# Low parts of the weights formed half a piece later, side tasks cut into shorter steps, sigmoids written as tanh in a one-core decoder trunk

## The chip, the cores and the metric

The kernel runs on one core of a Trainium2 chip. The metric is the device time of an execution in microseconds (us). In what follows PE is the matmul engine (PEld its weight loads), DVE the vector engine, ACT the scalar engine, POOL and SP the two engines that here mostly issue transfers. Each engine works through its own instructions in the order in which the program wrote them, and waits where an instruction needs what another engine has not finished.

## The reference

One layer of a hybrid decoder trunk on 256 tokens of width 2048, all in float32:

```python
hn = rms_norm(h, ln_gain)
z = split_columns(hn @ w_in + b_in)                # 2048 x 15904 weights
y_a = rglru_branch(z['lru_x'], ...) * silu(z['lru_gate'])
y_b = nsa_branch(...) * silu(z['nsa_gate'])        # sparse attention, 8 heads
y_c = fox_branch(...) * silu(z['fox_gate'])        # forgetting attention, 8 heads
mg = sigmoid(z['merge'])
merged = mg[0] * (y_a @ w_branch[0]) + mg[1] * (y_b @ w_branch[1]) + mg[2] * (y_c @ w_branch[2])
h = h + merged @ w_out
h = h + sigmoid(h @ w_ple_gate) * rms_norm(p @ w_ple, ple_gain)
```

The recurrence of the first branch, per channel, is what one part of the change rewrites:

```python
rec = sigmoid(ub @ wa + ba);  inp = sigmoid(ub @ wx + bx)
log_a = -8 * rec * softplus(-lam);  a = exp(log_a)
drive = sqrt(-expm1(2 * log_a)) * (inp * uc)
hseq[t] = a[t] * hseq[t-1] + drive[t]
```

## The kernel before

The time goes into streaming all weights through PE once. `plan()` cuts them into 384 pieces of 128 x 1024 numbers (some are 816 or 544 wide). For each piece, in the order of the plan:

- SP issues its transfer into one of `RAW` = 5 buffers `raw` (`issue`), up to `LOADS` = 6 pieces ahead in the program; a transfer waits until the buffer's earlier piece has been read.
- `cut` splits it for matmuls in a reduced float format (float32r): ACT copies it into the high part `wh`, DVE subtracts and writes the low part `wl`. Both have `AHEAD` + 1 = 4 buffers, so `wh` of piece i+3 can be written once PE has finished with piece i-1. `cut` is called at the start of piece i for piece i+3.
- `by_rows` gives PE twelve matmuls of 512 columns (`mm3`: activations' high part by `wh`, by `wl`, and their low part by `wh`; two row tiles, two contraction steps). The results build up in four PSUM tiles `main`.

Everything else (the recurrence, norms, turning of tiles, both attentions, the products with gates, the splits of their results) is written as Python generators, the side tasks: `lru_task`, `nsa_task`, `fox_task`, `y_split` and others. `Side.tick()` lets each running task emit its instructions up to its next `yield`; it is called in the middle of a piece's matmuls (in `by_rows`) and at the end of each piece. A tick stops when the planner's own clock puts DVE or ACT further behind PE than `LIMITS` allows. So the order on each engine is fixed when the program is built, and the side tasks' instructions stand between the `wh` and `wl` instructions of successive pieces. Side tasks' matmuls write four PSUM tiles `bank`; the last of them end at about 639 us, and after that only gates, splits and norms are left beside the weights.

Names used below: `k_lru` are the recurrence's tiles, `spc` and `spn` columns of its constants, `k_zt` a turned tile, `k_mg` the merge gate (formed by DVE from `main`, then a tanh on ACT, right after a merge chunk's last piece), `k_yh` and `k_yl` the split of a branch's result that the next product's matmuls read, `k_fx` the split of one forgetting head's query and key. A helper (line 206) records every operation, so all rows of the trace carry L206.

Of the kernel before, what the change touches and what calls it, by code (L numbers as in the profile page):

```python
# [12 lines left out]
AF = mybir.ActivationFunctionType  # L13
OP = mybir.AluOpType
# [309 lines left out]
def block_kernel(ctx: ExitStack, tc: tile.TileContext, io):  # L324
# [81 lines left out]
            Q.dma_start(h["raw"][:, a:b],  # L406
                        bass.AP(tensor=wsrc.tensor, offset=wsrc.offset + h["off"] + a, ap=[[m, P], [1, b - a]]))

    def cut(h, k=0, nk=None):
        m, n = h["nk"] * h["n"], h["n"]  # L410
        nk = nk or h["nk"]
        if k == 0:
            h["whl"] = [wp.tile([P, 1024], R32, tag=x, bufs=AHEAD + 1, name=nm(x)) for x in ("wh", "wl")]
        wh, wl = h["whl"]
        for a, b in parts_of(h, k, nk):
            split(wh[:, a:b], wl[:, a:b], h["raw"][:, a:b])
        h["wh"] = wh[:, :m].rearrange("p (k n) -> p k n", n=h["n"])
        h["wl"] = wl[:, :m].rearrange("p (k n) -> p k n", n=h["n"])

# [7 lines left out]
    def by_rows(h, x):  # L427

        if h["first"]:
            turn[0] ^= 1  # L430
            turns[h["kind"], h.get("what"), h["key"]] = turn[0]
        n = h["n"]
        out = [mains[2 * turn_of(h) + t][:, :n] for t in range(NT)]
        steps = [(h, t, k) for t in range(NT) for k in range(h["nk"])]
        if h is halves[0] or h is halves[1]:
            steps.sort(key=lambda x: x[2])
        if h is halves[-2]:
            return out
        if h is halves[-1]:

            steps = [(g, t, k) for t in range(NT) for g in halves[-2:] for k in range(g["nk"])]
        if h is halves[0]:

            (hi, lo), cuts = x(0), parts_of(h, 0, 1)
            for ws, last in (("wh", 0), ("wl", 1)):
                for a, b in cuts:
                    for t in range(NT):
                        T.matmul(out[t][:, a:b], hi[:, t * P:(t + 1) * P], h[ws][:, 0, a:b],
                                 start=a == 0 and not last, stop=False)
            for t in range(NT):  # L450
                T.matmul(out[t], lo[:, t * P:(t + 1) * P], h["wh"][:, 0, :], start=False, stop=False)
            steps = steps[NT:]
        for j, (g, t, k) in enumerate(steps):
            ts = slice(t * P, (t + 1) * P)
            if 2 * j == len(steps):
                side.tick()
            hi, lo = x(g["k"] + k)
            mm3(out[t], hi[:, ts], lo[:, ts], g["wh"][:, k, :], g["wl"][:, k, :], g["first"] and k == 0,
                g["last"] and k == g["nk"] - 1)
        return out  # L460
# [127 lines left out]
            split(hi[:, k, :], lo[:, k, :], x_tile(2 * i + k), x0[:, S + 2 * i + k:S + 2 * i + k + 1])  # L588

    def vec_task():  # L590
        a = VEC["lru_gate"]
        V.tensor_scalar(vec[:, a:], vec[:, a:], 0.5, None, op0=OP.mult)
        nl = sml([P, 8], name="nl")
        V.tensor_scalar(nl, vec[:, VEC["lam"]:VEC["lam"] + 8], -1.0, None, op0=OP.mult)
        yield from softplus(spc, nl, 8)
        V.tensor_scalar(spn, spc, -8.0, None, op0=OP.mult)
        V.tensor_scalar(spc, spc, 8.0, None, op0=OP.mult)

        V.scalar_tensor_tensor(gqn, vcol("nq"), SCALE, vcol("nk"), op0=OP.mult, op1=OP.mult)
        V.scalar_tensor_tensor(gqf, vcol("fq"), SCALE, vcol("fk"), op0=OP.mult, op1=OP.mult)  # L600
        yield True
# [123 lines left out]
    def lru_task(i):  # L725
        yield from side.wait("vec", f"lru_x{i // 2}")
        yield from side.room(k2=4, k4=1)
        u = st["u"]
        uc = two([P, 2, S], name="uc")


        ucs = [two([P, 2, S], R32, name="ucs") for _ in range(2)]
        wd = two([P, 2, 2, P], name="wd")
        G.dma_start(wd, io["wd"][:, 2 * i:2 * i + 2])
        for c in range(2):
            ct = 2 * i + c
            V.tensor_scalar(uc[:, c, :], u[:, ct, :], vcol("conv_w", 4 * ct + 3), vcol("conv_b", ct),
                            op0=OP.mult, op1=OP.add)
            for s in (1, 2, 3):
                V.scalar_tensor_tensor(uc[:, c, s:], u[:, ct, :S - s], vcol("conv_w", 4 * ct + 3 - s),  # L740
                                       uc[:, c, s:], op0=OP.mult, op1=OP.add)
            yield True
        own, other = (slice(0, 64), slice(64, P)), (slice(64, P), slice(0, 64))
        for c in range(2):
            for s in range(2):
                A.activation(ucs[c][own[s], s, :], uc[own[s], c, :], AF.Copy)
            for s in range(2):
                V.tensor_tensor(ucs[c][other[s], s, :], uc[own[s], c, :], f(ucs[c][own[s], s, :]), op=OP.subtract)
            yield True
        wds = mid([P, 2, 2, 2, P], R32, name="wds")  # L750
        wdh, wdl = wds[:, 0], wds[:, 1]
        split(wdh, wdl, wd)
        yield from side.settle()
        bs = yield from side.take(2)
        for c in range(2):
            for s in range(2):

                g = banks[bs[c]][:, s * S:(s + 1) * S]
                T.matmul(g, wdh[:, c, s, :], ucs[c][:, s, :], start=True, stop=False)
                T.matmul(g, wdl[:, c, s, :], ucs[c][:, s, :], start=False, stop=True)  # L760
        side.give(k4=1)
        yield True
        rec, inp, th = (two([P, 2, S], name="lru") for _ in range(3))
        for c in range(2):
            ct = 2 * i + c
            for s in range(2):
                g = banks[bs[c]][:, s * S:(s + 1) * S]
                A.activation(rec[own[s], c, :], g[own[s]], AF.Sigmoid, bias=vcol("ba", ct)[own[s]])
                A.activation(inp[own[s], c, :], g[other[s]], AF.Sigmoid, bias=vcol("bx", ct)[other[s]])
        side.back(*bs)  # L770
        yield True
        for c in range(2):
            ct = 2 * i + c
            A.activation(th[:, c, :], rec[:, c, :], AF.Tanh, scale=spc[:, ct:ct + 1])
        for c in range(2):
            ct = 2 * i + c
            A.activation(rec[:, c, :], rec[:, c, :], AF.Exp, scale=spn[:, ct:ct + 1])
        V.tensor_tensor(inp, inp, uc, op=OP.mult)
        yield True

        A.activation(uc, rec, AF.Square)
        V.scalar_tensor_tensor(th, uc, 1.0, th, op0=OP.add, op1=OP.mult)
        yield True
        A.activation(th, th, AF.Sqrt)
        V.tensor_tensor(th, th, inp, op=OP.mult)
        yield True
        for c in range(2):
            V.tensor_tensor_scan(st["yl"][:, 2 * i + c, :], rec[:, c, :], th[:, c, :], 0.0, op0=OP.mult, op1=OP.add)
        side.give(k2=4)
        yield True  # L790
# [106 lines left out]
    def nsa_task(g, pr, t):  # L897
# [19 lines left out]
        def soft(a, sc):  # L917

            for i, (o, x, msk) in enumerate(zip((pc[:, a, :], ps[:, a, 0, :], ps[:, a, 1, :]), sc,
                                                (cmask[:, t, :], mask[:, P * (2 - n):2 * P], mask[:, P:P + n * P]))):  # L920
                V.tensor_tensor_reduce(o, x, msk, -1.0, FLOOR, OP.add, OP.min, m[:, a, i:i + 1])
            for i, (o, x) in enumerate(((pc[:, a, :], pc[:, a, :]), (cell[:, a, 0], cells(ps[:, a, 0, :])),
                                        (cell[:, a, 1], cells(ps[:, a, 1, :])))):
                A.activation(o, x, AF.Exp, bias=m[:, a, i:i + 1], scale=-1.0, accum_out=s[:, a, i:i + 1])

        if t == 0:
# [3 lines left out]
            yield True  # L930
            for a in range(2):
                x = banks[bs[a]]
                soft(a, (x[:, 128:144], x[:, 144:272], x[:, :128]))
                side.back(bs[a])
                yield True
        else:
            for a in range(2):
# [1 line left out]
                mm3(banks[b0][:, :272], qh[:, a, :], ql[:, a, :], kh[:, g, :272], kl[:, g, :272], True, True)  # L939
                mm3(banks[b1][:, :256], qh[:, a, :], ql[:, a, :], kh[:, g, 272:], kl[:, g, 272:], True, True)  # L940
                yield True
                soft(a, (banks[b0][:, 256:272], banks[b1][:, :256], banks[b0][:, :256]))
                side.back(b0, b1)
                yield True
        side.give(k1=2)
# [4 lines left out]
        for a in range(2):  # L950
            V.tensor_scalar(pc3[:, a, :].rearrange("p (i c) -> p i c", i=3)[:, :, :16],
                            pc[:, a, None, :].to_broadcast([P, 3, 16]), s[:, a, 0:1], None, op0=OP.mult)
            for w in range(2):
                V.tensor_scalar(cell[:, a, w], cell[:, a, w], s[:, a, 1 + w:2 + w], None, op0=OP.mult)
        pt = pz.rearrange("p b n j -> p (b n j)")
        yield from cross(pt, pt, p)
        side.give(**{size: 1})
# [304 lines left out]
    def prepare(j):  # L1262
# [12 lines left out]
    for i, h in enumerate(halves):  # L1275
# [36 lines left out]
        else:  # L1312
            kv = h["key"]
            if h["first"] and kv == 0:
                st["cmpb"] = side.free.pop(0)[0]
            for k in range(h["nk"]):
                for q, w in enumerate((h["wh"], h["wl"])):
                    T.matmul(banks[st["cmpb"]][:4 * NCMP, kv * HID:(kv + 1) * HID], st["xs"][kv][:, h["k"] + k, :],
                             w[:, k, :], start=h["first"] and k == 0 and q == 0 and kv == 0,
# [21 lines left out]
        if halves[min(i + 3, len(halves) - 1)]["kind"] == "ple" and "pTs" not in st:  # L1341
            st["pTs"] = pTh, pTl = two([P, 2, S], R32, name="pTh"), two([P, 2, S], R32, name="pTl")
            split(pTh, pTl, st["pT"])
        for name in h["starts"]:
            start(name)
        side.tick()
# [14 lines left out]
MARGIN = 1600.0  # L1361

LAND = 5500.0
LIMITS = ((3500.0, 2500.0), (4000.0, 3500.0))

CMP_FROM = 17

# [74 lines left out]
```

## Time and profile before

| | us |
|---|---|
| median of 3 runs (1073.91 to 1074.62) | 1074.49 |
| the profiled execution | 1074.18 |
| its span, first to last instruction | 1072.4 |
| PE busy | 1059.0 |
| DVE busy | 771.2 |
| ACT busy | 617.4 |

Matmuls are pipelined: one of 512 columns shows as 0.39 us of busy time, and the next one starts before it ends. So PE is marked idle only where a matmul comes later than the drain of the one before it, and the distance from start to start tells more than the idle time. The granted clock is 1.0 of full speed in every stretch of work.

### The profile page before, as it was taken

To read this page: it belongs to the slowest core of one execution; us is meant where nothing else is said; L and a number is where in the kernel's file an instruction comes from. 1 tells how busy PE (TensorE), PEld (TensorE's weight loads), DVE (VectorE), ACT (ScalarE), POOL (GpSimd) and SP (SyncE) were. 2 spreads that over 40 slices of the span, in tenths; PEclk is the share of its full clock that TensorE was granted. 3 is DMA by queue.
4 is the path that set the end of the run, shared out by engine and by line. 5 is a ranking of instruction groups with operands and counts; after the bars stand their busy time and mean duration, and the time that the engine had idled before them with its cause. 6 is when DMAs were issued, how large, how long until landed. Compare 5 with 4: busy or idle time off the path is not lost.

```text
span 1072.4 us, 14101 instructions
## 1 busy us (share of the span) xinstructions
PE 1059.0 (99%) x4943; PEld 881.2 (82%) x4943; DVE 771.2 (72%) x1139; ACT 617.4 (58%) x917; POOL 51.1 (5%) x77
## 2 busy tenths in 40 slices
PE   9999999999999999999999999999999999999998
PEld 7887789887878878887888888888888888888886
DVE  7777699877787777778886866555776567666664
ACT  7668986776665565645645544465555444444442
POOL 0000000000000000001010000000000100000000
PEclk9999999999999999999999999999999999999999
DMA  9757768776666667558676776766676876788762
GB/s 340 251 186 220 255 219 266 243 240 193 214 206 195 198 200 221 159 172 281 201 224 210 226 217 184 236 216 204 206 255 199 264 248 212 228 253 262 264 215 79
DMA packets 86151, 237.54 MB, mean 222 GB/s; under 512 B 14008, under 2 KB 31040, under 8 KB 86080
## 3 DMA queue, kind: packets, MB, share of 16 engines
q1 hardware_dynamic: 81360, 220.89, 63.4%
q0 software_dynamic: 4720, 15.76, 5.7%
q8 instruction: 38, 0.62, 0.2%
q14 instruction: 33, 0.27, 0.1%
HBM read 215.62 MB, written 4.20 MB: 205 GB/s over the span
## 4 chain that ended last, share of the span: by engine, by line
PE 89%; ACT 4%; DVE 3%; DMA 2%; issue 2%; SPq 0%; DVEq 0%; ACTq 0%
PE main L206 85%; PE bank L206 4%; DVE wl L206 2%; ACT wh L206 2%; ACT k_lru L206 1%; DMA raw<-in_w 1%; DMA k_zn<-k_zt 1%; ACT L206 1%; SPq L206 0%; DVE k_zn L206 0%; ACT k_yh L206 0%; DVE k_fq L206 0%; DVE k_qn L206 0%; DVE k_zt L206 0%; DVE k_fin L206 0%
## 5 line engine op out<-in xcount | busy, mean ns | idle before, releaser
L206 DVE TENSOR_TENSOR wl<-raw,wh 128x1024 fp32r<-128x1024 f32 (+2 forms) x388 | 459.2, 1199 | 235.5 <-ACT wh L206 234.3
L206 ACT ACTIVATE wh<-raw 128x1024 fp32r<-128x1024 f32 (+2 forms) x388 | 397.9, 1039 | 291.3 <-PE main L206 258.4
L206 PE MATMUL main<-wh,k_hnh 128*128 128x512 f32 (+2 forms) x1026 | 395.8, 386 | 1.8 <-ACT wh L206 1.7
L206 PE MATMUL main<-wl,k_hnh 128*128 128x512 f32 (+2 forms) x1026 | 393.5, 384 | 3.4 <-DVE wl L206 3.3
L206 PE MATMUL main<-wh,k_hnl 128*128 128x512 f32 (+1 forms) x1024 | 392.7, 384 | 0.0
L206 PEld LDWEIGHTS main<-wl,k_hnh 128*128 128x128 f32 x1026 | 192.6, 188 | 41.6 <-DVE wl L206 6.5
L206 PEld LDWEIGHTS main<-wh,k_hnh 128*128 128x128 f32 x1026 | 193.0, 188 | 39.4 <-ACT wh L206 3.8
L206 PEld LDWEIGHTS main<-wh,k_hnl 128*128 128x128 f32 x1024 | 192.3, 188 | 37.7
L206 PE MATMUL main<-wl,k_yh 128*128 128x512 f32 x192 | 75.0, 391 | 1.0 <-DVE wl L206 1.0
L206 PE MATMUL main<-wh,k_yh 128*128 128x512 f32 x192 | 75.1, 391 | 0.5 <-ACT k_yh L206 0.5
L206 PE MATMUL main<-wh,k_yl 128*128 128x512 f32 x192 | 75.0, 390 | 0.0
L206 PE MATMUL main<-wh,k_mtl 128*128 128x512 f32 x128 | 49.9, 389 | 0.0
L206 PE MATMUL main<-wh,k_hth 128*128 128x512 f32 x128 | 49.8, 389 | 0.0
L206 PE MATMUL main<-wh,k_mth 128*128 128x512 f32 x128 | 49.8, 389 | 0.0
L206 PE MATMUL main<-wl,k_mth 128*128 128x512 f32 x128 | 49.8, 389 | 0.0
L206 PE MATMUL main<-wl,k_hth 128*128 128x512 f32 x128 | 49.8, 389 | 0.0
L206 PE MATMUL main<-wh,k_htl 128*128 128x512 f32 x128 | 49.8, 389 | 0.0
L206 PEld LDWEIGHTS main<-wl,k_yh 128*128 128x128 f32 x192 | 36.1, 188 | 9.0 <-DVE wl L206 1.7
L206 PEld LDWEIGHTS main<-wh,k_yh 128*128 128x128 f32 x192 | 36.1, 188 | 8.4 <-ACT k_yh L206 0.9
L206 PEld LDWEIGHTS main<-wh,k_yl 128*128 128x128 f32 x192 | 36.1, 188 | 7.9 <-DVE k_yl L206 0.4
L206 ACT ACTIVATE k_mg<-k_mg 128x512 f32<-128x512 f32 x24 | 15.2, 633 | 29.5 <-DVE k_mg L206 29.1
L206 PEld LDWEIGHTS main<-wh,k_htl 128*128 128x128 f32 x128 | 24.0, 188 | 5.0
(240 smaller groups left out, 957.0 us busy)
## 6 DMA issues: line engine op xcount, KB each, us to landing
raw<-in_w SPq DMA_DIRECT2D x369, 512.0 KB, 4.4
bias<-in_b_in POOLq DMA_DIRECT2D x21, 256.0 KB, 4.8
raw<-in_w SPq DMA_DIRECT2D x8, 408.0 KB, 3.8
k_pz<-k_prob SPq DMA_DIRECT2D x16, 128.0 KB, 3.9
e_dram<-k_e POOLq DMA_DIRECT2D x4, 512.0 KB, 3.7
k_merged<-k_zt SPq DMA_DIRECT2D x16, 128.0 KB, 2.9
k_xc<-in_x POOLq DMA_DIRECT2D x4, 512.0 KB, 5.2
k_hx<-k_zt SPq DMA_DIRECT2D x16, 128.0 KB, 3.0
```

What stands on the lines that cost most here:

```text
L206: r = call(out, *args, **kw)
```

## The change

Four edits. (1) From piece 14 on, `cut` emits ACT's copy at once but puts DVE's subtraction into a list `due`, which `low_parts()` empties in the middle of a piece, after the tick there, and at the end of each piece. (2) The recurrence's two sigmoids become tanh of half the argument, with the factors folded into `spc`, `spn`, the biases and the square root, and the sequence that read them is adapted. (3) Three more `yield`s cut the steps of `lru_task` and `nsa_task`, and one bank is given back earlier. (4) The second pair of `LIMITS` goes from (4000, 3500) to (3000, 2500).

```diff
+    due = []
+    def low_parts():
+        while due:
+            V.tensor_tensor(*due.pop(0), op=OP.subtract)
-    def cut(h, k=0, nk=None):
+    def cut(h, k=0, nk=None, late=False):
...
-            split(wh[:, a:b], wl[:, a:b], h["raw"][:, a:b])
+            if late:
+                A.activation(wh[:, a:b], h["raw"][:, a:b], AF.Copy)
+                due.append((wl[:, a:b], h["raw"][:, a:b], f(wh[:, a:b])))
+            else:
+                split(wh[:, a:b], wl[:, a:b], h["raw"][:, a:b])
...
             if 2 * j == len(steps):
                 side.tick()
+                low_parts()
...
-        V.tensor_scalar(spn, spc, -8.0, None, op0=OP.mult)
-        V.tensor_scalar(spc, spc, 8.0, None, op0=OP.mult)
+        V.tensor_scalar(spn, spc, -4.0, None, op0=OP.mult)
+        V.tensor_scalar(spc, spc, 4.0, None, op0=OP.mult)
...
-                A.activation(rec[own[s], c, :], g[own[s]], AF.Sigmoid, bias=vcol("ba", ct)[own[s]])
-                A.activation(inp[own[s], c, :], g[other[s]], AF.Sigmoid, bias=vcol("bx", ct)[other[s]])
-        side.back(*bs)
-        yield True
+                A.activation(rec[own[s], c, :], g[own[s]], AF.Tanh, bias=vcol("ba", ct)[own[s]], scale=0.5)
+                A.activation(inp[own[s], c, :], g[other[s]], AF.Tanh, bias=vcol("bx", ct)[other[s]], scale=0.5)
+            side.back(bs[c])
+            yield True
...
-            A.activation(th[:, c, :], rec[:, c, :], AF.Tanh, scale=spc[:, ct:ct + 1])
+            A.activation(th[:, c, :], rec[:, c, :], AF.Tanh, scale=spc[:, ct:ct + 1], bias=spc[:, ct:ct + 1])
...
-            A.activation(rec[:, c, :], rec[:, c, :], AF.Exp, scale=spn[:, ct:ct + 1])
-        V.tensor_tensor(inp, inp, uc, op=OP.mult)
+            A.activation(rec[:, c, :], rec[:, c, :], AF.Exp, scale=spn[:, ct:ct + 1], bias=spn[:, ct:ct + 1])
+        V.scalar_tensor_tensor(inp, inp, 1.0, uc, op0=OP.add, op1=OP.mult)
...
-        A.activation(th, th, AF.Sqrt)
+        A.activation(th, th, AF.Sqrt, scale=0.25)
...
                 V.tensor_tensor_reduce(o, x, msk, -1.0, FLOOR, OP.add, OP.min, m[:, a, i:i + 1])
+            yield True
...
-            cut(halves[j])
+            cut(halves[j], late=j > EARLY + AHEAD)
...
+        low_parts()
         for name in h["starts"]:
...
-LIMITS = ((3500.0, 2500.0), (4000.0, 3500.0))
+LIMITS = ((3500.0, 2500.0), (3000.0, 2500.0))
```

How this moves instructions shows best at three places. The first is ACT in the recurrence, from its exponentials to the gates of the next pair of banks. Before, with the tables that ACT must load (the rows that ended the burst at 115.85 us):

```order
L206 ACT_TABLE_LOAD
L206 ACTIVATE k_lru_984<-k_lru_984,spn 128x256 x2
L206 ACT_TABLE_LOAD
L206 ACTIVATE k_lru_1080<-bank_89,vec 64x256
L206 ACTIVATE k_lru_1081<-bank_89,vec 64x256
L206 ACTIVATE k_lru_1080<-bank_89,vec 64x256
L206 ACTIVATE k_lru_1081<-bank_89,vec 64x256
L206 ACTIVATE k_lru_1080<-bank_87,vec 64x256
L206 ACTIVATE k_lru_1081<-bank_87,vec 64x256
L206 ACTIVATE k_lru_1080<-bank_87,vec 64x256
L206 ACTIVATE k_lru_1081<-bank_87,vec 64x256
L206 ACTIVATE wh_1093<-raw_1009 128x1024
```

After, from the `wh` ahead of the same exponentials:

```order
L206 ACTIVATE wh_1034<-raw_962 128x1024
L206 ACTIVATE k_lru_975<-k_lru_973,spc 128x256 x2
L206 ACTIVATE k_lru_973<-k_lru_973,spn 128x256 x2
L206 ACTIVATE k_lru_1063<-bank_89,vec 64x256
L206 ACTIVATE k_lru_1064<-bank_89,vec 64x256
L206 ACTIVATE k_lru_1063<-bank_89,vec 64x256
L206 ACTIVATE k_lru_1064<-bank_89,vec 64x256
L206 ACTIVATE wh_1072<-raw_996 128x1024
L206 ACTIVATE k_uc_676<-k_lru_973 128x512
L206 ACTIVATE wh_1092<-raw_1010 128x1024
L206 ACTIVATE wh_1106<-raw_1032 128x1024
```

Both table loads are gone from this place, the eight activations of the next task are four, and the next `wh` comes after eight instructions where there were twelve, counted from the exponentials' group on.

The second is DVE ahead of a merge gate `k_mg`, around 340 us. Before, from a `wl` through the end of a sparse head's softmax (`sp_sm`, `k_pz`) to the gate:

```order
L206 TENSOR_TENSOR wl_3231<-raw_3139,wh_3230 128x1024
L206 TENSOR_TENSOR k_pct_3246<-bank_87,k_pct_3246 32x256
L206 TENSOR_SCALAR sp_sm_3176<-sp_sm_3176 128x6
L206 RECIPROCAL sp_sm_3176<-sp_sm_3176 128x6
L206 TENSOR_TENSOR sp_sm_3176<-sp_sm_3176,bg 128x6
L206 TENSOR_SCALAR k_pc_546_3178<-sp_pc_3177,sp_sm_3176 128x3x16
L206 TENSOR_SCALAR k_pz_3181<-k_pz_3181,sp_sm_3176 128x4x32 x2
L206 TENSOR_SCALAR k_pc_546_3178<-sp_pc_3177,sp_sm_3176 128x3x16
L206 TENSOR_SCALAR k_pz_3181<-k_pz_3181,sp_sm_3176 128x4x32 x2
L206 STREAM_TRANSPOSE k_prob_3180<-k_pz_3181 128x512
L206 TENSOR_TENSOR wl_3262<-raw_3157,wh_3261 128x1024
L206 SCALAR_TENSOR_TENSOR k_mg_3277<-main_85,rsr,bias_3109 128x512
```

After, the rows ahead of the same gate:

```order
L206 TENSOR_TENSOR wl_3191<-raw_3103,wh_3190 128x1024
L206 TENSOR_TENSOR k_pct_3212<-bank_89,k_pct_3212 32x256
L206 TENSOR_TENSOR wl_3218<-raw_3132,wh_3217 128x1024
L206 TENSOR_TENSOR wl_3247<-raw_3164,wh_3246 128x1024
L206 TENSOR_TENSOR k_pt_3289<-k_pz_3056,k_pt_3288 128x512
L206 TENSOR_TENSOR k_ql_3293<-k_qn_2133,k_qh_3292 128x256
L206 TENSOR_TENSOR wl_3280<-raw_3188,wh_3279 128x1024
L206 TENSOR_TENSOR k_pct_3329<-bank_90,k_pct_3329 32x256
L206 TENSOR_TENSOR wl_3308<-raw_3215,wh_3307 128x1024
L206 SCALAR_TENSOR_TENSOR k_mg_3339<-main_85,rsr,bias_3169 128x512
L206 SCALAR_TENSOR_TENSOR k_mg_3340<-main_86,rsr,bias_3169 128x512
```

The softmax steps of a head no longer stand here: between the last three low parts and the gate there is one `k_pct`, and before them two splits (`k_pt`, `k_ql`).

The third is DVE ahead of the first forgetting head, at 504 us. Before:

```order
L206 SCALAR_TENSOR_TENSOR k_fv_4691<-main_86,rsr,bias_4570 128x4x128
L206 TENSOR_TENSOR wl_4715<-raw_4651,wh_4714 128x1024
L206 TENSOR_TENSOR k_fx_4727<-k_fq_4334,k_fx_4726 128x256
L206 SCALAR_TENSOR_TENSOR k_fx_4729<-k_fk_4563,gqf,k_fx_4728 128x128 x2
L206 SCALAR_TENSOR_TENSOR k_fbias_4748<-k_nck_4724,cq,cst 128x128
L206 SCALAR_TENSOR_TENSOR k_fbias_4748<-k_nck_4724,cq,cst 128x256
L206 TENSOR_TENSOR wl_4754<-raw_4673,wh_4753 128x1024
```

After:

```order
L206 SCALAR_TENSOR_TENSOR k_fv_4692<-main_86,rsr,bias_4579 128x4x128
L206 TENSOR_TENSOR wl_4697<-raw_4638,wh_4696 128x1024
L206 TENSOR_TENSOR k_fx_4727<-k_fq_4378,k_fx_4726 128x256
L206 SCALAR_TENSOR_TENSOR k_fx_4729<-k_fk_4546,gqf,k_fx_4728 128x128 x2
L206 TENSOR_TENSOR wl_4716<-raw_4656,wh_4715 128x1024
L206 SCALAR_TENSOR_TENSOR k_fbias_4749<-k_nck_4724,cq,cst 128x128
L206 SCALAR_TENSOR_TENSOR k_fbias_4749<-k_nck_4724,cq,cst 128x256
```

The low part of the piece whose `wh` was issued just before stood ahead of `k_fx`; now it stands behind it.

On all engines together, PE, POOL and SP have the same number of instructions as before, DVE has one more (a 128x16 scaling near the start), and ACT has six table loads fewer (9 for 15).

## Rows read from the trace of the kernel before

**Rows 1.** The page's head: busy time, share of the span, instructions of each engine.

```profile
PE 1059.0 (99%) x4943; PEld 881.2 (82%) x4943; DVE 771.2 (72%) x1139; ACT 617.4 (58%) x917; POOL 51.1 (5%) x77
```

**Rows 2.** Busy time by stretch: length, then busy us (x instructions), PEclk, DMA, GB/s.

```profile
97.00:119.00 22.00, 19.23 (x92) 15.12 (x91) 9.55 (x9) 20.80 (x32) 0.29 (x1) 1.00 0.61 196
119.00:640.00 521.00, 517.18 (x2535) 433.55 (x2534) 411.82 (x732) 326.43 (x546) 32.74 (x46) 1.00 0.69 217
640.00:1060.00 420.00, 420.00 (x1855) 347.86 (x1854) 269.33 (x272) 202.41 (x237) 15.13 (x22) 1.00 0.71 225
```

**Rows 3.** PE's waits: for whom, us in total, times, longest us.

```profile
PE main L206 <- DVE wl L206: 4.3, 8, 0.8
PE main L206 <- ACT wh L206: 1.7, 3, 0.7
PE main L206 <- ACT k_yh L206: 0.5, 1, 0.5
PE bank L206 <- DVE k_fx L206: 0.5, 2, 0.2
```

**Rows 4.** PE's timeline: start us, us, instruction [idle before <-releaser].

```profile
103.89 0.39 PE L206 MATMUL main<-wh,k_hnl 128*128 128x512 f32 x1
104.87 0.50 PE L206 MATMUL main<-wh,k_hnh 128*128 128x512 f32 x1 [0.60 <-ACT wh L206]
106.13 0.50 PE L206 MATMUL main<-wl,k_hnh 128*128 128x512 f32 x1 [0.76 <-DVE wl L206]
106.47 0.40 PE L206 MATMUL main<-wh,k_hnl 128*128 128x512 f32 x1
```

**Rows 5.** ACT's timeline around those stops.

```profile
97.87 0.69 ACT L206 ACTIVATE k_zt<-main,rsr 128x512 f32<-128x512 f32 x1 [1.65 <-PE main L206]
98.58 1.28 ACT L206 ACT_TABLE_LOAD   x1
99.87 3.87 ACT L206 ACTIVATE k_lru<-bank,vec 64x256 f32<-64x256 f32 x8
103.76 3.90 ACT L206 ACTIVATE wh<-raw 128x1024 fp32r<-128x1024 f32 x4
```

**Rows 6.** ACT's groups by shape: busy us, mean ns of one | idle before.

```profile
L206 ACT ACT_TABLE_LOAD x15 | 19.2, 1283 | 1.0 <-PEq L1435 0.7
...
L206 ACT ACTIVATE k_hnh<-k_xT,x 128x256 fp32r<-128x256 f32 x15 | 6.9, 497 | 0.4 <-DMA k_xT<-in_xT 0.4
...
L206 ACT ACTIVATE k_qh<-k_qn 128x256 fp32r<-128x256 f32 x8 | 3.1, 402 | 0.0
```

**Rows 7.** DVE's longest wait in total: us, times, longest us.

```profile
DVE wl L206 <- ACT wh L206: 234.3, 187, 6.9
```

**Rows 8.** DVE's timeline before PE's stop at 346 us.

```profile
336.65 1.23 DVE L206 TENSOR_TENSOR wl<-raw,wh 128x1024 fp32r<-128x1024 f32 x1 [2.79 <-ACT wh L206]
...
342.11 1.41 DVE L206 SCALAR_TENSOR_TENSOR k_mg<-main,rsr,bias 128x512 f32<-128x512 f32 x2
345.17 1.23 DVE L206 TENSOR_TENSOR wl<-raw,wh 128x1024 fp32r<-128x1024 f32 x1 [1.65 <-ACT wh L206]
```

**Rows 9.** ACT's timeline in the same stretch.

```profile
342.90 1.29 ACT L206 ACTIVATE k_mg<-k_mg 128x512 f32<-128x512 f32 x2 [5.06 <-DVE k_mg L206]
```

**Rows 10.** ACT's timeline, before PE's stops at 181 and 311 us.

```profile
177.52 1.28 ACT L206 ACTIVATE kk<-k_zn,gqn 128x128 fp32r<-128x128 f32 x4 [3.62 <-DMA k_zn<-k_zt]
...
310.36 0.63 ACT L206 ACTIVATE k_yh<-k_yl 128x512 fp32r<-128x512 f32 x1 [2.08 <-DVE k_yl L206]
```

**Rows 11.** DVE's timeline before PE's stop at 505 us.

```profile
503.59 1.23 DVE L206 TENSOR_TENSOR wl<-raw,wh 128x1024 fp32r<-128x1024 f32 x1 [0.83 <-ACT wh L206]
504.74 0.42 DVE L206 TENSOR_TENSOR k_fx<-k_fq,k_fx 128x256 fp32r<-128x256 f32 x1
```

**Rows 12.** ACT's waits for weights to land: us, times, longest us.

```profile
ACT wh L206 <- DMA raw<-in_w: 2.9, 9, 0.5
```

**Rows 13.** The page's DMA issues: count, KB each, median us to landing.

```profile
raw<-in_w SPq DMA_DIRECT2D x369, 512.0 KB, 4.4
```

More of the change, by code (lines that the diff above doesn't have):

```diff
@@ L590, in vec_task @@
     def vec_task():
-        a = VEC["lru_gate"]
-        V.tensor_scalar(vec[:, a:], vec[:, a:], 0.5, None, op0=OP.mult)
+        for cols in (slice(VEC["ba"], VEC["lam"]), slice(VEC["lru_gate"], N_VEC)):
+            V.tensor_scalar(vec[:, cols], vec[:, cols], 0.5, None, op0=OP.mult)
         nl = sml([P, 8], name="nl")
@@ L932, in nsa_task @@
                 x = banks[bs[a]]
-                soft(a, (x[:, 128:144], x[:, 144:272], x[:, :128]))
+                yield from soft(a, (x[:, 128:144], x[:, 144:272], x[:, :128]))
                 side.back(bs[a])
@@ L941, in nsa_task @@
                 yield True
-                soft(a, (banks[b0][:, 256:272], banks[b1][:, :256], banks[b0][:, :256]))
+                yield from soft(a, (banks[b0][:, 256:272], banks[b1][:, :256], banks[b0][:, :256]))
                 side.back(b0, b1)
@@ L954, in nsa_task @@
                 V.tensor_scalar(cell[:, a, w], cell[:, a, w], s[:, a, 1 + w:2 + w], None, op0=OP.mult)
+        yield True
         pt = pz.rearrange("p b n j -> p (b n j)")
@@ L1316, in block_kernel @@
             for k in range(h["nk"]):
+                if 2 * k == h["nk"]:
+                    low_parts()
                 for q, w in enumerate((h["wh"], h["wl"])):
@@ L1343, in block_kernel @@
             split(pTh, pTl, st["pT"])
+        low_parts()
         for name in h["starts"]:
```

## The prediction

> **What bounds the kernel now.** I read the page's head first: PE is busy for 1059.0 of 1072.4 us [rows 1], so the other engines matter only where they stop PE. Then the stretches [rows 2]: from 640 to 1060 us PE is never idle and runs 1855 matmuls in 420.0 us, 0.2264 us from start to start. That is its pace for 512 columns, and a piece of twelve takes 2.72 us. Between 97 and 119 us PE is idle for 22.00 - 19.23 = 2.77 us, between 119 and 640 us for 521.00 - 517.18 = 3.82 us. The waits [rows 3] say for what: fourteen stops, eight for a low part `wl`, three for a high part `wh`, one for `k_yh`, two for `k_fx`; one `wh` and one `wl` of them belong to the program's opening, which the change leaves alone, so twelve lie here: two `wh` and two `wl` in the first stretch, eight in the second.
>
> An idle mark understates a stop. In [rows 4] the third matmul after that at 103.89 should start 3 x 0.226 = 0.68 us later, at 104.57, and starts at 106.47: 1.90 us lost where 0.60 + 0.76 = 1.36 are marked, so 0.27 per stop come on top (drain and restart). With that the first stretch loses 2.77 + 4 x 0.27 = 3.85 us and the second 3.82 + 8 x 0.27 = 5.98 us. [...]
>
> **Where the stops come from.** The first four are the recurrence's. ACT reads `k_zt` at 97.87, loads a table for 1.28 us, works off eight sigmoids in 3.87 us, and only at 103.76 comes to the `wh` that PE wants [rows 5]. A second burst, with two loads (the first place shown in the section on the change), lies behind the other two stops, and the recurrence's last burst behind one `wl` of the second stretch.
>
> Most of the others are queues. DVE stands in front of a `wl` waiting for its `wh` for 234.3 us in 187 waits, 6.9 us at the longest [rows 7]; all side work behind it stands too. Up to 336.65 DVE waits 2.79 us for such a `wh`; it is never idle from there to the merge gate `k_mg`, which starts at 342.11 with no wait marked, so its inputs were there before [rows 8]; ACT stands 5.06 us in front of its tanh of `k_mg` [rows 9] with the next `wh` behind it; and the `wl` at 345.17 [rows 8] ends after PE wants it. The next merge gate has a stop of the same pattern. Two late `k_fx` come of a `wl` put ahead of them: DVE waits 0.83 us, spends 1.23 on it, and starts `k_fx` at 504.74 [rows 11], which PE waits for [rows 3]. The late `k_yh` is ACT's at 310.36, which waited 2.08 us for DVE's product [rows 10]; two more `wl` are late behind the second branch's split, squeezed into four pieces. A transfer takes a small part too: ACT waits 3.62 us for `k_zn` [rows 10], and what PE loses behind it is in the second stretch's idle time without a row among [rows 3]; I put it at 0.2 + 0.27 = 0.5 us, the smallest mark there with its restart.
>
> So the second stretch's 3.82 us divide into 0.5 for `k_yh`, 0.5 for two `k_fx`, 0.2 for the transfer and 2.6 for five `wl`: 0.52 each, 0.79 with restart.
>
> **The change, part by part.**
>
> Tanh for sigmoid. Six of fifteen table loads go: 6 x 1.283 = 7.7 us of ACT [rows 6]. Sixteen activations get a bias column beside their scale column. No row has both; a column costs 497 - 402 = 95 ns (one column against none at 256 columns [rows 6]), so the second costs 0 to 95 ns; I take 95, 1.5 us in all, hidden in ACT's idle time (617.4 of 1072.4 us are busy [rows 1]). [...] What enters is the burst: with four of the eight activations ahead of `k_zt`, ACT has after it 0.69 + 4 x 0.48 = 2.6 us of work and reaches `wh` at about 100.5 instead of 103.76, 3.3 us earlier where 1.9 were missing. At 116 us two loads (2.6 us) and four activations (1.9 us) leave the burst, 4.5 where about 1.95 were missing. So **the first stretch's 3.85 us go**, and one `wl` of the second with them, 0.8 us.
>
> Late low parts. `wl` of piece i+3 is emitted half a piece (1.36 us) later and behind the tick's work. PE reads it after 2.5 pieces, 6.8 us; less its own 1.23 us, DVE may be 5.6 us behind before PE notices. The cover is that lead; if it goes, each late `wl` costs a stop, 0.76 + 0.27 = 1.03 us at the longest mark [rows 3]. In return DVE no longer stands at `wl` while ACT is just starting on `wh`, and side work gets the 234 us. The two `k_fx` come 0.83 + 1.23 = 2.06 us earlier at most, not at all at least (if their own ACT halves come no earlier), where 0.25 + 0.27 = 0.5 each were missing; I take the first, four times what is wanted: 1.0 us go. The merge gates come earlier by up to the 2.79 us of the wait, where the two stops miss 0.79 each: 1.6 us go.
>
> Shorter steps and the tighter limit. They cost no instruction but put fewer side instructions between two `wh`. In the new order the fourth `k_yh` of the first branch stands three pieces earlier, and the second branch's split no longer falls into four successive pieces. The three stops there cost 0.5 + 0.27 and twice 0.79: 2.4 us go, or nothing if the steps meet others instead (the second rival). DVE's one instruction more, on 16 columns, is shorter than the 0.42 us of a `k_fx` of 256 [rows 11], in idle time.
>
> The refill. A `raw` buffer is read out half a piece later, so SP issues its next transfer at least 1.36 us later. Five buffers turn around in 5 x 2.72 = 13.6 us; `wh` 3.90 / 4 = 0.98 [rows 5], the half piece 1.36, `wl` 1.23 and a landing of 4.4 us [rows 13] take 8.0, leaving 5.6. ACT waited for landings 2.9 us in all, 0.5 at the longest [rows 12], with three pieces of lead to PE. I take nothing; the upper bound is the slow rival's.
>
> **Sum.** 3.85 + 0.8 + 1.0 + 1.6 + 2.4 = 9.6 us. The transfer's 0.5 I leave in. New stops cannot be priced in a trace that does not have them: 0 at best, and at worst as many again. The longest pile-ups left in the new order are about 3 us of DVE work against the 5.6 and 2.6 us of ACT work, so I take three small stops of 0.2 + 0.27, 1.4 us. Net 8.2: 1074.2 (the profiled execution; the runs' median is 0.3 above it) - 8.2 = **1066.0 us**.
>
> **Rivals.**
>
> Only the recurrence is cured. Fewer loads and shorter bursts take 3.85 + 0.8 us, and the queue stops move to other pieces, since every side instruction is still there (DVE 411.82 us in 119 to 640 us [rows 2]): 1069.5 us. For it: these stops sit where steps of several tasks happened to meet, and the order changes everywhere. Against: DVE's largest wait is what is removed [rows 7].
>
> No change: the four early stops go, and about as much returns as new ones, 1074 us. The tighter limit delays side work, and a result that PE wants (a split, a forgetting head's query) comes late more often. Against: the chain of side work stands earlier in the new order, not later.
>
> Slower: low parts late. If DVE is more than 5.6 us behind where several tasks meet, the `wl` behind the tick stops PE at 1.03 us each. Ten such stops eat the gain, and one in eight of the 190 pieces between 119 and 640 us, 24 stops, costs 24.7 - 8.2 = 16.5 us more than before: 1091 us; fifteen stops would be 1081.5. In favour: DVE is 79% busy there (411.82 of 521.00). Against: nowhere in the new order do I find the needed pile.
>
> **How the numbers follow.** The forecast, 1064 to 1068.3 us: 0.67. Better still, below 1064 (the restart being dearer than 0.27): 0.05. Recurrence only, 1068.3 to 1071.8: 0.17. No change: 0.06. Slower: 0.05. This kernel's runs agree within 0.07%, and I take 0.2%, 2.1 us, as what can be told from no change; faster then has 0.67 + 0.05 + 0.17 = 0.89. From 1063.5 to 1070.0 us lie the forecast, most of the better case and half of the second: about 0.8.
>
> **What will show it.** Right: PE's idle time between 97 and 119 us near zero, nine table loads, DVE's waits for `wh` at `wl` well below 234 us, at most a handful of PE waits after 10 us, PE busy for all but some 7 us of the span, and the stretch from 640 us unchanged. Wrong: PE waiting for `wl` more than eight times, or ACT waiting for `raw` by more than 10 us; then the low parts or the refill came too late. If the idle time between 119 and 640 us stays near 3.8 us, the queue stops only moved.

## The result, and the profile after

The changed kernel took 1067.6 us (median of 4 runs, 1066.82 to 1068.0), the kernel before 1074.2 beside it: a ratio of 0.9938, 95% interval 0.9922 to 0.9954. A second set of runs gave 1067.5 us. The forecast was 1066.0, in a range from 1063.5 to 1070.0. The profiled execution took 1067.73 us, its span is 1066.0 for 1072.4 [rows 1].

The page's head of the changed kernel, then busy time by stretch (length, then PE, PEld, DVE, ACT and POOL busy us with instructions, PEclk, DMA share, GB/s):

```profile
PE 1056.6 (99%) x4943; PEld 881.7 (83%) x4943; DVE 771.6 (72%) x1140; ACT 612.9 (57%) x911; POOL 49.1 (5%) x77
```

```profile
97.00:119.00 22.00, 22.00 (x114) 18.59 (x113) 13.79 (x17) 20.38 (x35) 0.00 (x0) 1.00 0.79 250
119.00:640.00 521.00, 518.26 (x2544) 436.20 (x2543) 412.93 (x730) 324.65 (x539) 30.73 (x46) 1.00 0.70 217
640.00:1060.00 420.00, 420.00 (x1855) 347.77 (x1854) 264.82 (x269) 200.64 (x236) 15.17 (x22) 1.00 0.70 222
```

Against [rows 2] the first stretch has no idle time left (114 matmuls in it for 92), the last one is unchanged to the matmul, and the middle one went only from 3.82 to 521.00 - 518.26 = 2.74 us. What PE still waits for, outside the opening, and the waits of DVE and ACT that the forecast named (engine, for whom, us, times, longest):

```profile
PE main L206 <- DVE wl L206: 2.7, 5, 1.5
```

```profile
DVE wl L206 <- ACT wh L206: 180.6, 149, 2.5
```

```profile
ACT wh L206 <- DMA raw<-in_w: 3.7, 4, 2.2
```

Twelve stops in [rows 3] became five, all for `wl`; no `k_fx`, no `k_yh` is waited for. DVE stands 180.6 us at `wl` for 234.3 [rows 7]. So the sum's large terms came, and something new stands for `wl`. PE's timeline shows the longest of the five (start us, us, instruction, idle before), and DVE's what was ahead of that `wl`:

```profile
162.45 0.28 PE L206 MATMUL main<-wh,k_hnh 128*128 128x272 f32 x1
164.26 0.39 PE L206 MATMUL main<-wl,k_hnh 128*128 128x272 f32 x1 [1.53 <-DVE wl L206]
```

```profile
158.70 1.35 DVE L206 TENSOR_TENSOR wl<-raw,wh 128x544 fp32r<-128x544 f32 x2
159.97 2.07 DVE L206 TENSOR_TENSOR k_zn<-k_z,sp_nss 128x512 f32<-128x512 f32 x2
162.07 1.25 DVE L206 STREAM_TRANSPOSE k_zt<-k_zn 128x1024 f32<-128x1024 f32 x1
163.24 3.02 DVE L206 TENSOR_TENSOR wl<-raw,wh 128x816 fp32r<-128x816 f32 x3
```

Here the matmuls have 272 columns and start 0.125 us apart: the pieces are 544 and 816 wide, and PE is through one in 12 x 0.125 = 1.5 or 18 x 0.125 = 2.3 us, not 2.72. DVE's side work is as long as ever, two ticks of it stand ahead of a late `wl`, and it is never idle. PE gets ahead of it.

### The profile page after: what moved, and what is told of

It reads as the page before. It is cut to its first block, busy times and chain, and to the rows that moved or that the text cites. A ratio compares the mean times of both kernels' runs of the same rounds, so it can differ in the third digit from the quotient of the medians.

```text
span 1066.0 us, 14138 instructions
## 1 busy us (share of the span) xinstructions
PE 1056.6 (99%) x4943; PEld 881.7 (83%) x4943; DVE 771.6 (72%) x1140; ACT 612.9 (57%) x911; POOL 49.1 (5%) x77
## 4 chain that ended last, share of the span: by engine, by line
PE 95%; DVE 2%; issue 1%; ACT 1%; DMA 1%; SPq 0%; DVEq 0%
PE main L206 90%; PE bank L206 5%; DVE wl L206 1%; DMA raw<-in_w 0%; SPq L206 0%; ACT wh L206 0%; DMA k_zn<-k_zt 0%; DVE k_zn L206 0%; ACT k_lru L206 0%; DVE k_qn L206 0%; DVE k_fin L206 0%; ACT kk L206 0%; DVE k_uc L206 0%; DVE k_z L206 0%; DVE k_yl L206 0%
## 5 line engine op out<-in xcount | busy, mean ns | idle before, releaser
L206 DVE TENSOR_TENSOR wl<-raw,wh 128x1024 fp32r<-128x1024 f32 (+2 forms) x388 | 460.0, 1197 | 181.5 <-ACT wh L206 180.6
L206 PEld LDWEIGHTS main<-wh,k_mth 128*128 128x128 f32 x128 | 24.0, 188 | 5.0
```

Source lines behind the costliest of these rows:

```text
L206: r = call(out, *args, **kw)
```

## The experiments

Theory A is the prediction's, corrected by this trace: each part removes stops of its own, and late low parts cost something where pieces are narrow. Theory B says that the tanh alone is the gain; theory C that a later read of `raw` delays the refill. All times below are medians, beside 1074.1 to 1074.6 us for the kernel before in the same sets.

**One part at a time.** The tanh without the rest (`inp` alike, and the factors in `spc`, `spn`, `vec`, `th` as in the change):

```diff
-                A.activation(rec[own[s], c, :], g[own[s]], AF.Sigmoid, bias=vcol("ba", ct)[own[s]])
+                A.activation(rec[own[s], c, :], g[own[s]], AF.Tanh, bias=vcol("ba", ct)[own[s]], scale=0.5)
...
```

> The kernel before with the recurrence's sigmoids written as tanh and nothing else (9 table loads for 15). Theory A, that each part of the change removes stops of its own: the four stops of PE between 97 and 119 us go and one wl after it, 3.85 + 0.8 us, so 1074.2 - 4.65 = 1069.5 us (1068.9 to 1070.5), and of PE's waits between 119 and 640 us the two for k_fx, the one for k_yh and those for wl behind the merge gates stay. Theory B, that the tanh alone is the whole gain and the rest only reshuffles the order: 1067.6 us as the changed kernel, within 0.6.

It took 1070.78 us (ratio 0.9969, 0.9959 to 0.9979). Busy time in two stretches, and PE's waits:

```profile
97.00:119.00 22.00, 21.78 (x111) 18.09 (x110) 13.13 (x14) 20.38 (x36) 0.54 (x1) 1.00 0.75 238
119.00:640.00 521.00, 516.96 (x2535) 434.33 (x2534) 410.86 (x731) 322.40 (x538) 33.56 (x46) 1.00 0.69 217
```

```profile
PE main L206 <- DVE wl L206: 3.3, 8, 0.8
...
PE bank L206 <- DVE wl L206: 0.8, 1, 0.8
PE bank L206 <- DVE k_fx L206: 0.5, 2, 0.2
```

Theory B falls, and theory A is 0.3 us outside its range: 3.8 us are the tanh's, nearly all in the first stretch (2.77 us of idle time became 0.22). In the second, idle time did not fall (3.82 to 521.00 - 516.96 = 4.04 us). Most queue stops stay, the two `k_fx` with them; the one for `k_yh` went, which A had not said, and two longer ones for `wl` came at 179 and 181 us (0.76 and 0.83).

Late low parts without the rest (`low_parts` and its calls as in the change):

```diff
-            cut(halves[j])
+            cut(halves[j], late=j > EARLY + AHEAD)
...
```

> The kernel before with the low parts formed half a piece later and nothing else (sigmoids kept, 16 table loads). Theory A: the stops of the first stretch stay (3.85 us), those for k_fx and at the merge gates go (2.6 us), and in their place come stops for wl between 150 and 180 us, where the pieces are 816 and 544 wide and so short that the lead shrinks (3.3 us as in the changed kernel): about 1074.9 us, 1073.5 to 1076. Theory B: no stop is owed to the place of the low parts, 1074.2 within 0.6, with k_fx waited for as before. Theory C, that later reading of raw delays the refill: ACT's waits for landed weights grow from 2.9 us to over 6, and PE's stops come behind them; 1076 or more.

It took 1077.75 us (ratio 1.0039, 1.0026 to 1.0053): slower, by more than theories A and B said, and in the range of theory C. ACT's timeline, PE's, and busy time by stretch:

```profile
105.72 0.90 ACT L206 ACTIVATE k_lru<-k_lru,spc 128x256 f32<-128x256 f32 x2
106.64 1.28 ACT L206 ACT_TABLE_LOAD   x1
107.94 0.91 ACT L206 ACTIVATE k_lru<-k_lru,spn 128x256 f32<-128x256 f32 x2
108.85 1.28 ACT L206 ACT_TABLE_LOAD   x1
110.15 3.85 ACT L206 ACTIVATE k_lru<-bank,vec 64x256 f32<-64x256 f32 x8
114.02 3.90 ACT L206 ACTIVATE wh<-raw 128x1024 fp32r<-128x1024 f32 x4
```

```profile
112.48 0.39 PE L206 MATMUL main<-wh,k_hnl 128*128 128x512 f32 x1
115.13 0.50 PE L206 MATMUL main<-wh,k_hnh 128*128 128x512 f32 x1 [2.26 <-ACT wh L206]
116.39 0.50 PE L206 MATMUL main<-wl,k_hnh 128*128 128x512 f32 x1 [0.76 <-DVE wl L206]
...
117.30 0.63 PE L206 MATMUL main<-wl,k_hnh 128*128 128x512 f32 x1
117.73 0.63 PE L206 MATMUL main<-wh,k_hnl 128*128 128x512 f32 x1
```

```profile
117.00:121.00 4.00, 4.00 (x12) 3.13 (x11) 3.48 (x5) 4.00 (x9) 0.00 (x0) 0.57 0.85 247
```

The order moved, and ACT's second burst stands in one piece: 114.02 - 105.72 = 8.3 us without a `wh`. PE stops for 2.26 and 0.76 us, and then the granted clock is 0.57 of full speed from 117 to 121 us: matmuls start 117.73 - 117.30 = 0.43 us apart, 0.2 more than the 0.226 at clock 1.00, and 12 of them stand in these 4 us where 18 would fit. Here the stops cost more than themselves. `k_fx` is indeed waited for no more, but a `k_yh` is, for 1.8 us. ACT's waits for `raw` are 6.8 us in all: theory C's number, but not its place, since the long stops stand for `wh` behind ACT's burst and for `k_yh`.

**One part taken back.** All low parts at once, the rest as changed:

```diff
-            cut(halves[j], late=j > EARLY + AHEAD)
+            cut(halves[j])
```

> The changed kernel with every low part formed at once as before; tanh, shorter steps and limits stay. Theory A: the stops for wl between 150 and 180 us go (3.3 us), the two for k_fx and the two wl behind merge gates come back (2.6 us): 1067.6 - 0.7 = 1066.9 us, 1066 to 1068; DVE's waits for wh at wl go back up from 180.6 us to over 210. Theory B (the late parts neither help nor hurt, the stops depend on how the steps happen to meet): 1067.6 within 0.6 and no stop at k_fx or a merge gate. If the late parts are what cures the queues in the whole of 119 to 640 us: 1070 us or more.

It took 1067.05 us (1066.12 to 1068.21): no difference from 1067.6 that can be told. PE's waits and DVE's:

```profile
PE bank L206 <- DVE k_fx L206: 1.2, 2, 0.9
PE main L206 <- ACT wh L206: 1.1, 2, 0.7
PE main L206 <- DVE wl L206: 1.0, 2, 0.8
```

```profile
DVE wl L206 <- ACT wh L206: 230.2, 194, 4.3
```

As theory A has it, the stops among narrow pieces are gone and those for `k_fx` are back; the merge gates' stops, against it, are not back. Two stops at 178 to 180 us are longer, too (0.48 and 0.77 us for one of 0.43), and a `k_yh` is waited for, 0.3 us. So beside the other parts the late ones cure `k_fx` (1.2 us marked) and some 1.1 us more, and cost about what they cure: from 97 to 640 us PE is busy for 540.25 us without them and 540.26 with them.

The sigmoids put back with what belongs to them, the rest as changed:

```diff
-                A.activation(rec[own[s], c, :], g[own[s]], AF.Tanh, bias=vcol("ba", ct)[own[s]], scale=0.5)
+                A.activation(rec[own[s], c, :], g[own[s]], AF.Sigmoid, bias=vcol("ba", ct)[own[s]])
...
```

> The changed kernel with the recurrence's sigmoids put back (16 table loads for 9); late low parts, shorter steps and limits stay. Theory A, that the table loads make the stops of the recurrence: PE is idle again between 97 and 119 us, and the time goes up by 3 to 4.65 us, to 1070.6 to 1072.3. Rival, that it is the length of the burst and not the loads: the step of four activations instead of eight is enough, ACT's burst in front of a wh is 1.28 + 1.9 us for 1.28 + 3.87, no idle time returns there, and the time stays within 1 us of 1067.6.

It took 1071.03 us (1069.4 to 1075.03). Theory A has the time, the rival the place. Table loads, and the first stretch:

```profile
L206 ACT ACT_TABLE_LOAD x16 | 20.5, 1283 | 1.0 <-PEq L1454 0.7
```

```profile
97.00:119.00 22.00, 22.00 (x112) 18.35 (x111) 12.49 (x15) 21.77 (x37) 0.00 (x0) 1.00 0.76 237
```

With 16 loads PE is not idle between 97 and 119 us: in this order two `wh` stand between `k_zt` and the next eight sigmoids (ACT forms them from 99.96 us on), and that is enough there. The profiled execution is the fastest of the six (1069.4), 1.7 us above the changed kernel's 1067.73; its stops lie in the second stretch, 3.2 us for `wl` where the changed kernel has 2.7, and 0.5 for a `k_yh`. What the other runs lose beyond that no trace shows.

The three added yields and the early return of a bank taken out:

```diff
-            side.back(bs[c])
-            yield True
+        side.back(*bs)
+        yield True
...
-            yield True
...
-                yield from soft(a, (x[:, 128:144], x[:, 144:272], x[:, :128]))
+                soft(a, (x[:, 128:144], x[:, 144:272], x[:, :128]))
```

> The changed kernel without the three added yields and the early return of a bank; tanh, late low parts and limits stay. The tanh alone measured 1070.78 us and the changed kernel without late parts 1067.05, so shorter steps and limits are worth 3.7 us together. Theory A1, the steps carry most of it: 1069.5 to 1071 us, with stops again behind the branches' splits or the merge gates between 300 and 500 us. Rival A2, the tighter limit carries it: within 0.8 of 1067.6, and the next run is the slow one.

It took 1078.53 us, slower than the kernel before (ratio 1.0039, 1.0027 to 1.0052) and 11 us above the changed one. PE's timeline, ACT's ahead of it, the stretch behind it, and DVE's timeline ahead of the `k_yh`:

```profile
314.00 0.39 PE L206 MATMUL main<-wh,k_yl 128*128 128x512 f32 x1
318.90 0.79 PE L206 MATMUL main<-wh,k_yh 128*128 128x512 f32 x1 [4.51 <-ACT k_yh L206]
```

```profile
308.67 1.29 ACT L206 ACTIVATE k_mg<-k_mg 128x512 f32<-128x512 f32 x2 [2.74 <-DVE k_mg L206]
309.87 2.95 ACT L206 ACTIVATE wh<-raw 128x1024 fp32r<-128x1024 f32 x3
312.73 0.49 ACT L206 ACTIVATE k_th<-k_zt,vec 128x256 f32<-128x256 f32 x1
...
318.22 0.63 ACT L206 ACTIVATE k_yh<-k_yl 128x512 fp32r<-128x512 f32 x1 [1.09 <-DVE k_yl L206]
```

```profile
319.00:324.00 5.00, 5.00 (x13) 3.82 (x14) 2.21 (x14) 4.01 (x14) 0.00 (x0) 0.50 0.20 79
```

```profile
317.16 0.42 DVE L206 SCALAR_TENSOR_TENSOR k_gn<-k_th,k_gn 128x256 f32<-128x256 f32 x1 [0.37 <-ACT k_gn L206]
317.50 0.69 DVE L206 TENSOR_TENSOR k_yl<-k_yl,k_gl 128x512 f32<-128x512 f32 x1
```

The last `k_yh` of the first branch comes behind the merge gate `k_mg`, four `wh` and the eight activations that begin with `k_th`. What it waits for at the end, 1.09 us, is its product `k_yl`, which in DVE's order (the last fence) stands behind four products `k_gn` that wait for those activations. PE waits 4.5 us, and then goes through 13 matmuls in 5 us at clock 0.50. Three more stops for `wl`, of 1.35, 1.58 and 0.63 us at 194, 223 and 430 us, are a smaller part of the 11 us. Both theories missed: the steps carry far more than A1's 1069.5 to 1071 us.

The limits put back:

```diff
-LIMITS = ((3500.0, 2500.0), (3000.0, 2500.0))
+LIMITS = ((3500.0, 2500.0), (4000.0, 3500.0))
```

> The changed kernel with the second pair of limits put back to (4000, 3500); the rest stays. Theory A2, the tighter limit carries the 3.7 us: 1069.5 to 1071 us, with stops again where several steps stand between two low parts. Theory A1 (the steps carry it): within 0.8 of 1067.6. In both the stops for wl between 156 and 164 us stay, since they come of the late parts.

It took 1067.84 us, as the changed kernel, and the stop of 1.5 us for `wl` is there again. But with the low parts at once as well, so that tanh and steps alone are left:

```diff
-            cut(halves[j], late=j > EARLY + AHEAD)
+            cut(halves[j])
...
-LIMITS = ((3500.0, 2500.0), (3000.0, 2500.0))
+LIMITS = ((3500.0, 2500.0), (4000.0, 3500.0))
```

> Tanh and shorter steps alone: the changed kernel with every low part at once and the old limits. The tanh alone measured 1070.78, with steps and limits 1067.05, and the limits made no difference beside late parts (1067.84 for 1067.6). Theory A, the steps are the second gain by themselves: 1067.05 within 0.8. Rival, without late parts the limit matters: 1068.5 to 1070.8, with a stop for wl near 380 or 475 us as with the tanh alone.

It took 1071.53 us (ratio 0.9973, 0.9963 to 0.9984). Its rival was right, though the time is 0.7 us above its range and the stop another than it named. PE's wait, and DVE's timeline ahead of it:

```profile
PE main L206 <- ACT k_yh L206: 3.4, 1, 3.4
```

```profile
304.06 3.50 DVE L206 TENSOR_TENSOR wl<-raw,wh 128x1024 fp32r<-128x1024 f32 x3 [1.65 <-ACT wh L206]
307.48 0.69 DVE L206 TENSOR_TENSOR k_yl<-k_yl,k_gl 128x512 f32<-128x512 f32 x1
```

Once more the split of the first branch comes behind the merge gate: its product `k_yl` stands on DVE behind three `wl`, the first of which waited for the `wh` behind ACT's `k_mg`. Where that one `k_yh` falls decides 3 us and more, and steps, limits and late parts all move it. So the worth of a part hangs on the others: under the old limits the late parts take 3.7 us off (1071.53 to 1067.84), under the tighter ones nothing, and the tighter limits take 4.5 us off without late parts (1071.53 to 1067.05) and 0.2 with them.

**The narrow pieces.** Late parts for pieces 1024 wide alone; then with `k_zn`'s transfers on POOL's queue too (`q` is POOL's for `k_zn` alone):

```diff
-            cut(halves[j], late=j > EARLY + AHEAD)
+            cut(halves[j], late=j > EARLY + AHEAD and halves[j]["n"] == 512)
```

> The changed kernel with low parts late only for pieces 1024 wide; those of the 816 and 544 wide pieces at once. The wl that PE waited 1.53 us for stood behind the product k_zn (2.07 us) and its turn k_zt (1.25 us); in this order a wl stands between the two. Theory A, that the lead of a late low part is too short where pieces are short: the four stops of PE between 156 and 173 us go (0.38 + 0.22 + 1.69 + 0.39 = 2.7 us in excess of the cadence), k_fx is still not waited for, and the time is 1064.9 us (1064.2 to 1066). Rival, the transfers: the pieces behind k_zn's transfers land late whatever the low parts do, and as with all parts formed at once 1.7 us of stops stand at 178 to 180 us for the 0.6 of the changed kernel: 1066.0 or more. Rival, mere reshuffling: 1067 within 0.7, with as many stops elsewhere.

```diff
-            Q.dma_start(to[:, a, :], zt[32 * a:32 * a + 32].rearrange("p b n j -> p b (n j)"))
+            (q or Q).dma_start(to[:, a, :], zt[32 * a:32 * a + 32].rearrange("p b n j -> p b (n j)"))
```

> As the run before it, and the four transfers of k_zn issued by POOL for SP. SP spends 2.5 us on issuing them, and the weights' transfers stand behind them. Theory D, that this queue makes the stop at 178 us: that stop goes, ACT's waits for landed raw fall below 3 us, and the time is 0.5 to 1.5 us below the run before it. Rival: the transfers share the same engines whoever issues them, ACT waits for k_zn as long as before, and the time is the same within 0.5, or k_zn lands later and it is 0.5 to 1 us more.

They took 1070.27 and 1067.67 us. The first is a miss for theory A's number and the rival on transfers is right, at more than its price. SP's queue (issues), ACT's and PE's timeline of that run, and the stretch behind:

```profile
166.85 2.54 SPq L206 DMA_DIRECT2D k_zn<-k_zt  x4
169.49 15.97 SPq L206 DMA_DIRECT2D raw<-in_w  x9
```

```profile
177.40 1.06 ACT L206 ACTIVATE wh<-raw 128x1024 fp32r<-128x1024 f32 x1 [2.70 <-DMA raw<-in_w]
```

```profile
178.51 0.33 PE L206 MATMUL bank<-wh,k_xs 128*60 128x256 f32 x1 [0.38 <-ACT wh L206]
179.77 0.33 PE L206 MATMUL bank<-wl,k_xs 128*60 128x256 f32 x1 [0.93 <-DVE wl L206]
182.48 0.80 PE L206 MATMUL main<-wl,k_hnh 128*128 128x512 f32 x1 [1.44 <-DVE wl L206]
```

```profile
183.00:188.00 5.00, 5.00 (x13) 3.86 (x12) 4.49 (x7) 1.84 (x4) 0.54 (x1) 0.50 0.84 260
```

The stop of 1.53 us at 162 us is gone, as forecast. But the weights' transfers stand on SP behind the four of `k_zn`, which take 2.54 us to issue, a piece lands late, three stops follow one another, and again the clock falls: 13 matmuls in 5 us at clock 0.50, 9 fewer than the 22 that fit at 0.226 us each. With the four transfers on POOL the time was 2.6 us less, where 0.5 to 1.5 were expected, since the fall of the clock, 9 x 0.226 = 2.0 us of matmuls, went (the clock is 1.00 in every stretch from 97 to 640 us of that run). Theory D came only in part there: two stops are left, 0.30 and 1.12 us at 180 and 182 us, and ACT's waits for landed `raw` are 6.1 us for 6.2, not below 3.

**Late parts where they help.** From piece 140 on, then with POOL's queue as well:

```diff
-            cut(halves[j], late=j > EARLY + AHEAD)
+            cut(halves[j], late=j >= 140)
```

> The changed kernel with low parts late only from piece 140 on (about 385 us), at once before it. Without late parts PE stopped at 178 us (0.65 + 1.03), at 308 us (0.43 + 0.16) and at k_fx at 498 and 570 us (0.23 + 1.23 + 0.42); with late parts everywhere k_fx was never waited for, and 3.3 us were lost among the narrow pieces. Theory A, that late parts are worth what stands at k_fx and cost what stands in narrow pieces: 1067.05 - 1.9 = 1065.2 us (1064.4 to 1066.2), no wait for k_fx. Rival, the k_fx stops have another cause (their own halves on ACT): they stay, 1067 within 0.7.

> As the run before it, with k_zn's four transfers issued by POOL, which beside late parts on wide pieces took 2.6 us (1070.27 to 1067.67). Theory D, that SP's queue holds the weights up there: the stops at 178 us (1.7 us) shrink by half at least, and the time is 0.8 to 1.7 us below the run before it, about 1064.0. [...]

They took 1065.63 (1064.77 to 1065.74) and 1064.26 us (1063.36 to 1065.04), ratios 0.9915 (0.9901 to 0.9929) and 0.9904 (0.989 to 0.9917), where 1065.2 and about 1064.0 were expected. PE's waits between 119 and 640 us in the first, then between 97 and 640 us in the second:

```profile
PE main L206 <- DVE wl L206: 0.8, 1, 0.8
PE main L206 <- ACT wh L206: 0.7, 1, 0.7
PE main L206 <- ACT k_yh L206: 0.3, 1, 0.3
```

```profile
PE main L206 <- ACT k_yh L206: 0.3, 1, 0.3
```

No `k_fx` in either, and on POOL's queue the two stops behind `k_zn`'s transfers (0.7 and 0.8 us above) are gone: one wait of 0.3 us is left. PE, DVE and ACT have the same instructions in the same order in both kernels, so the queue alone makes the difference, though the slowest run of the second is slower than the fastest of the first. In the second kernel these transfers are issued from 161.62 us on while SP goes on with the weights:

```profile
161.62 2.17 POOL L206 DMA_DIRECT2D k_zn<-k_zt  x4 [5.09 <-DVE k_zt L206]
```

The `wh` that waits longest for its weights there starts at 174.90 us, where in the first it starts at 177.37. Whether SP's time for issuing four transfers counts or their place ahead of the weights in the queue, these two runs do not separate.

The changed kernel once more, as a yardstick in the same set:

> The changed kernel itself once more, on the chip of these runs, as a yardstick for the differences of half a microsecond: 1067.6 within 0.7 by every theory.

It took 1067.5 us (1066.54 to 1069.2). The last version is 3.2 us below it and 10.3 below the kernel before.

## Why the prediction was right, and where its sum was off

**What bounds it, and the floor.** Right. The stretch from 640 us is unchanged. The prediction's two losses, 3.85 + 5.98 = 9.8 us, leave 1074.2 - 9.8 = 1064.4 us for the same matmuls at clock 1.00 [rows 2] without a stop, and 1064.26 us with one stop left stands by that. It is not a strict floor: the profiled execution of that version took 1063.36 us for the 1074.18 of the kernel before, 10.8 us less where 9.8 were counted. In the changed kernel PE is not busy for 1066.0 - 1056.6 = 9.4 us of the span, where some 7 were forecast.

**Tanh.** The stops of the first stretch went and their price held: 3.8 us by itself for 3.85 + 0.8. The second column cost what was taken: `k_lru<-k_lru,spc` went from 497 to 590 ns. Nine loads of 1283 ns are left. The rows show no time beside a load but its own: in the late-only kernel the load at 106.64 ends at 107.92 and the next activation starts at 107.94, and the one ahead of the load ended at 106.62; the load of [rows 5] stands as close. But the reason was too narrow: sigmoids in the new order stop nothing in that stretch. What stopped PE was a burst of ACT without a `wh`, of which loads were a part.

**Late low parts.** This term was wrong. It was credited with 2.6 us, 1.0 at `k_fx` and 1.6 at the merge gates. The `k_fx` stops are its own (they return without it, at 1.2 us marked); the merge gates' stops stay away without it. Beside the other parts it brings nothing measurable (1067.05 for 1067.6 us).

**The step that was wrong is the lead of 5.6 us**, with the new stops sized from it. It was worked out from pieces of 2.72 us; among narrow pieces, of 1.5 and 2.3 us, two and a half pieces are 3.8 to 5.7 us, less about 1 for the `wl` itself. A pile of some 3 us of DVE's work, which the prediction held to be harmless, stands just there: `k_zn` and its turn (2.07 + 1.25), with two more `wl` ahead of it. New stops came to more than was put down: left over were to be 0.5 + 1.4 = 1.9 us; left are 2.7 us marked and five restarts of 0.27, 4.1 us. Those 2.2 us more cover the 1.6 by which the time missed.

**Steps and limits.** 2.4 us were put down, 3.7 measured (1070.78 to 1067.05), but not by the working: they are not the sum of three small stops, nor of two parts. Steps without limits or late parts gain nothing (1071.53), the limits alone beside late parts nothing (1067.84 for 1067.6), and limits and late parts without the steps lose (1078.53).

**The total.** It came nearer than its parts. Along one way through the runs, tanh gave 3.8 us for 4.65, steps and limits 3.7 for 2.4, and late parts with their new stops -0.5 for 2.6 - 1.4 = 1.2. The second error makes up for part of the other two, and that is luck.

**The refill.** Nothing was taken, and ACT's waits for `raw` went from 2.9 to 3.7 us. What the prediction did not see is that SP's queue holds weights up behind `k_zn`'s transfers: 1.4 us (1065.63 to 1064.26) with late parts from piece 140 on; in the changed kernel itself this was not tried.

**The rivals.** Recurrence only, at 1069.5 us, is what one gets without the rest (1070.78), and its thought that stops move to other pieces is half true of the changed kernel: those of before are gone, but for the 3.82 us of idle time in the second stretch there are 2.74, nearly all in new places. The slow one has its mechanism in small, five `wl` too late; in full it did not come here. Late parts with long bursts do make the kernel slower (1077.75), but through an ACT burst, the clock and a late `k_yh`, not through many late `wl`.

Open stays why runs of the kernel with sigmoids reach to 1075 us: only its fastest run was profiled. That one `k_yh` costs 1.8, 3.4 and 4.5 us in the three versions where it comes late is shown; that the planner could be made to place it early by rule was not tried.

## What to carry to other kernels

A lead that is counted in pieces is short in time where pieces are small: size a deferral for the smallest one, or leave those out. In an order made by a planner, parts of a change don't add: run each part alone and each part taken back, and look for the one late result (here a split behind a merge gate) that several of them move. When an engine in order is held up, look at every queue that its input passed, transfers of other work on the same issuing engine included.

## What the runs showed of the hardware

PE's clock fell in four of the profiled executions, though from 97 to 1060 us PE is busy in them for 953.05 to 959.17 of 963 us: after 2.26 and 0.76 us of idle time (late-only) it was granted at 0.57 between 117 and 121 us, after 4.51 us (old steps) at 0.50 between 319 and 324, after three stops of 0.38, 0.93 and 1.44 us one behind the other (late parts for wide pieces) at 0.50 between 183 and 188, after 3.44 us (tanh and steps alone) at 0.64 between 309 and 311.5. Matmuls of 512 columns then start 0.42 to 0.43 us apart (117.30 and 117.73, 319.50 and 319.92, 183.07 and 183.50, 310.57 and 311.00), for 0.226 at clock 1.00. In the kernel before, a pair of stops of 0.60 and 0.76 us [rows 4] left the clock at 1.00 [rows 2], and behind the single stop of 1.53 us in the changed kernel it is 1.00 from 164 to 169 us. So in these runs the small stops cost themselves and a restart (the single one 164.26 - 162.45 - 0.125 = 1.69 us for 1.53 marked), while the stop of 4.51 us and the three close together were each followed by 13 matmuls in 5 us, where 22 fit at the full clock. How long or how close stops must be for the clock to fall, these runs do not show.
